# Reordered attention steps, a hand-written order for the memory projection and one low part moved in a decoder-trunk kernel

## The chip, the cores and the metric

The kernel runs on one core of a Trainium2 chip. The metric is the device time of one execution in microseconds (us), and lower is better. The kernel before took 1815.08 us (median of three runs, 1813.99 to 1815.76).

The engines are named as in the profile. PE is the matrix engine and PEld its weight loads, which run beside its matmuls. DVE is the vector engine, ACT the scalar engine, POOL the GpSimd engine. SP issues most of the DMAs. PSUM is the accumulator memory that PE writes.

## The reference, cut to what matters

One inference step of one decoder layer for a prompt of 1024 rows and eight samples of four rows (all float32):

```
h = rms_norm(x) @ w_in                      # u | v | q latent | kv latent | rope key
a = chunk_gmlp(u, v)                        # group A
b = softmax(q k^T / sqrt(96)) v             # group B: 8 heads of 64+32; prompt and samples
x = x + concat(norm(a), norm(b)) @ w_o      # output projection
hm = rms_norm(mem_prompt, g_mem_in)         # 256 memory rows of 1024
mk = rms_norm(hm @ w_mk per head of 128, g_mk)   # output o_mk
mv = hm @ w_mv                                   # output o_mv
x = x + mem_attend(rms_norm(x), mk, mv)
x = x + (silu(conv(gate)) * val) @ w_down   # gate, val = rms_norm(x) @ w_up
```

Three places of this computation are touched: the prompt's attention in group B, the stretch in which mk and mv are computed while the last of the eight sample batches finishes its softmax, and the beginning of the down projection.

## The kernel before

**Products.** A float32 product is made of three PE passes over two-part operands. `split` (lines 192 to 210) makes the high part with a cast on ACT (L200, or L204 with a gain) and the low part as a subtraction on DVE (L201, or L207 with a gain). `mm3` (line 179) issues high times high, high times low, low times high. Where `self.lows` is a list, the low parts are kept back and `flush` issues them later. Most instructions are L185 (`mm3`), L200 and L201, whatever the stage.

**Order.** A planner orders most instructions. Inside a `manual_schedule` block the named engines run in the order in which the program text issues them; `behind(a, b)` puts instruction a behind b in the plan.

**Prompt attention (phase2a, lines 780 to 850).** All engines but SP run in hand order. The work is twelve units of a head and a half of the prompt, each with three or four steps. One step issues in this order: the transposes of exponentials (`trans`, L1031, with a copy on ACT, L1033), the `outs` of earlier units, the scores of a later unit (`scores`, L1009 to L1020: three matmuls into PSUM, a masked maximum on DVE at L1014 or L1018, a multiplication by the row's root at L1020; the exponential L1023 runs on ACT), the low parts kept back, the products with the values (`value`, L1046), and `extra` work for this step. The `outs` hold the copy of a unit's output out of PSUM with a reciprocal (L1053, L1054 on DVE) and its transposes. The two buffers `s` of PSUM are refilled by the scores after the maxima have read them. The norms of q and k (`proj_group`, with `rsqrt_steps` at lines 238 to 270: eleven short operations) are cut into seven steps that stand in `extra`; the last of them multiplies k by its root (L960).

**Memory's stretch (phase2b, lines 1300 to 1322, and mem_kv, line 1579).** Here only SP runs in hand order; PE, ACT and DVE are ordered by the planner. The last sample batch's softmax (`batch_softmax`, line 1462, thirteen parts: norm steps on POOL, scaling, maxima at L1479, a broadcast through PE at L1508 and L1516, a subtraction at L1528, the exponential at L1524) and its products with the cache (`quad_pv`, L1537) interleave with four heads of `hm @ w_mk` (L1605, 24 matmuls each), sixteen units of `hm @ w_mv` (L185, output tile v) and the norms:

```
for h in range(4):
    for i in range(2):
        nc.tensor.matmul(st[:, 2 * h + i : 2 * h + i + 1], sq[h][:, i * P : i * P + P], self.ones[:, :1], ...)   # L1636
...
    nc.tensor.matmul(st[:, 8 + i : 9 + i], acc[z][:, i * P : i * P + P], self.ones[:, :1], ...)                  # L1639
...
    nc.vector.tensor_scalar(dg, self.ident, r[:, h, i : i + 1], None, ALU.mult)                                  # L1657
    nc.tensor.matmul(bc[:, i * P : i * P + P], self.ones, dg, start=True, stop=True)                             # L1658
```

The memory rows are split by `g_mem_in` into mh and ml (L204, L207) just ahead of the first head. The squares of the memory rows are summed by two reduces (L1617). The weights come through `stream` (line 1566): a DMA issued by SP into one of three buffers `raw`, a cast on ACT, a low part on DVE.

**Output projection (mixed, line 1712, and out_proj, line 1755).** `mixed` loads the weight w_o and the mixed rows; `tail` holds the three closing steps of the last sample batch (L1545, L1549, L1561), and `end` the product with w_uv (L1328). `out_proj` runs `end` and then the chunks (0,0), (0,1) and so on.

**Down projection (ffn_down, line 2468, unit, line 2413).** `unit` splits one weight block into high and low; the last piece of the stage before adds PSUM to kept sums (`place`, L2366 and L2368) and so frees the PSUM buffers that the first products d need.

Of the kernel before, what the change touches and what calls it, by code (L numbers as in the profile page):

```python
# [153 lines left out]
class Net:  # L154
# [83 lines left out]
    def rsqrt_steps(self, p, out, ss, scale, e=None, eps=EPS):  # L238
# [5 lines left out]
        x, q, y, a = (self.t(p, [P, n], d, f"rq{k}{n}", 2 if n < 100 else 1)[:w] for k, d in (("x", F32), ("h", F32), ("y", I32), ("a", F32)))  # L244
# [5 lines left out]
        for k in range(2):  # L250
            yield
            o = out if k else y
            if e is nc.vector:
# [6 lines left out]
                e.scalar_tensor_tensor(o, q, 5.0, y, ALU.add, ALU.mult)  # L260
# [411 lines left out]
    def phase2a(self):  # L672
# [75 lines left out]
        spread(tok_s, 4, 11)  # L748
# [4 lines left out]
        extra[2][:0] = preps[0][2:]  # L753
# [27 lines left out]
        with tc.manual_schedule(engines={E.PE, E.Activation, E.DVE, E.Pool}):  # L781
# [57 lines left out]
            for fs in [V] + [outs[t] for t in sorted(outs)] + [[]] * 4:  # L839
# [52 lines left out]
    def proj_group(self, p, pp, hf, i0, i1, s, c, tt=("tp", 4)):  # L892
# [77 lines left out]
        return [alloc] + qk + [lambda: next(it, 0)] * 7, [lambda i=i: part(i, 2) for i in range(i0, i1) if i < 8]  # L970
# [19 lines left out]
    def head_unit(self, p, pp, h, G, s, c):  # L990
# [7 lines left out]
        def scores(e):  # L998
# [9 lines left out]
            for z in range(nc_):  # L1008
# [3 lines left out]
                self.mm3(sv, [(qh[:, tq], ql[:, tq])], [(kh[:, kc], kl[:, kc])])  # L1012
# [166 lines left out]
    def phase2b(self):  # L1179
# [50 lines left out]
        at(last - 4, 3, lambda: self.split(*wk0, raws[0].rearrange("p (k n) -> p k n", k=8)))  # L1230
        for b in range(NB):
# [3 lines left out]
            for r, (k, pos) in enumerate(((12, 0), (13, 0), (14, 0), (14, 3) if b == NB - 1 else (15, 0), (15, 0) if b == NB - 1 else (15, 3), (16, 0), (17, 0), (17, 3), (18, 2), (19, 2), (20, 0), (21, 2), (22, 3))):  # L1235
                f = lambda b=b, r=r: self.batch_softmax(p, ppt, st[b], r, b == NB - 1)
                if n + k <= last:
                    at(n + k, pos, f)
                else:
                    late.append(f)  # L1240
# [15 lines left out]
        def steps(n0, n1):  # L1256
            for n in range(n0, n1):
# [27 lines left out]
                if 0 <= n < last:  # L1285
                    rope = (Q + 1, quads[Q + 1], st[(Q + 1) // 8]) if n % 2 and Q + 1 < NB * 8 else None
                    for f in self.pair_score(p, pp, n, quads[n // 2], st[n // 16], rope):
                        at(n + 1, -1, f)
# [12 lines left out]
        with tc.manual_schedule(engines={E.SP}):  # L1301
# [5 lines left out]
            mem = self.mem_kv(raws, wk0)  # L1307
            for f in late[:3]:
                f()
            next(mem)  # L1310
            steps(last + 1, last + 4)
            for _ in range(5):
                next(mem)
            steps(last + 4, last + 7)
            for f in late[3:]:
                f()
            for _ in range(6):
                next(mem)
            steps(last + 7, last + 16 + LAG)
            for _ in mem:  # L1320
                pass
# [140 lines left out]
    def batch_softmax(self, p, pp, s, r, final):  # L1462
# [28 lines left out]
        elif r == 4:  # L1491
            s["m"] = self.t(p, [P, 2, 32], F32, "mx", 2)
            peak(0, 0, 24)
        elif r == 5:
            s["it"] = norms(24, 32, nc.gpsimd if final else nc.vector)
# [6 lines left out]
        elif r == 8:  # L1502
            scale(nc.vector, 24, 32)
# [10 lines left out]
        elif r == 11:  # L1514
# [4 lines left out]
            if final:  # L1519
                self.less(nc.vector, s)  # L1520
# [20 lines left out]
    def batch_out(self, p, s, part, pp=None, final=False):  # L1541
        nc = self.nc
        if part == 0:
            s["oo"] = self.t(p, [P, 257], F32, "oo", 2)
            nc.scalar.copy(s["oo"], s["o"])  # L1545
# [33 lines left out]
    def mem_kv(self, raws, wk0):  # L1579
# [7 lines left out]
        mh, ml = (self.t(p, [P, 8, 256], FR, x) for x in ("mh", "ml"))  # L1587
        acc = [self.t(p, [P, 256], F32, f"acc{z}") for z in range(2)]
        mr = [r.rearrange("p (k n) -> p k n", k=4) for r in raws[1:3]]
        xs = [(mh[:, k], ml[:, k]) for k in range(8)]  # L1590
        kr, sq = [], []

        for h in range(4):
            w = wk0 if h == 0 else self.stream(I["w_mk"][h], 8, raw=raws[3].rearrange("p (k n) -> p k n", k=8) if h == 1 else None)
            if h == 1:
                self.behind(self.cast, cast)
            yield
            ps = self.t(pp, [P, 512], F32, "b", 2)[:, :256]
            pairs = ((0, 0), (1, 0)), ((0, 1),)
            for z in pairs if h == 0 else (((0, 0), (0, 1)), ((1, 0),)):  # L1600
                for k in range(8):
                    if h == 0 and z is pairs[0]:
                        cast = self.split(*xs[k], mr[k // 4][:, k % 4], self.col("g_mem_in", k))
                    for a, e in z:
                        nc.tensor.matmul(  # L1605
                            ps, w[a][:, k], xs[k][e], start=z[0] == (0, 0) and a + e + k == 0, stop=len(z) == 1 and k == 7
                        )
                    if h == 0 and z is pairs[0] and k % 2:
                        yield
            kr.append(self.t(p, [P, 256], F32, "kr", 4))  # L1610
            nc.scalar.copy(kr[h], ps)
            sq.append(self.t(p, [P, 256], F32, "sq", 4))
            nc.scalar.activation(sq[h], ps, AF.Square)
            yield
        for x, s2 in zip(mr, acc):
            nc.scalar.activation(x, x, AF.Square)
            nc.vector.tensor_reduce(s2, x.rearrange("p k n -> p n k"), AX.X, ALU.add)  # L1617
        yield
        av = [self.t(pp, [P, 512], F32, f"v{i}") for i in range(2)]

        def values(k):
            wh, wl = (x.rearrange("p k n -> p (k n)").rearrange("p (k n) -> p k n", k=2) for x in self.stream(I["w_mv"][k // 2], 8))
            for i in range(2):
                t = slice(i * P, i * P + P)
                x = self.mm3(av[i], [tuple(x[:, t] for x in xs[k + e]) for e in range(2)],
                             [(wh[:, e], wl[:, e]) for e in range(2)], first=k == 0, last=k == 6)
                if k == 4 and i == 0:
                    self.behind(x, self.spread)

        values(0)  # L1630
        yield
        values(2)
        yield
        for h in range(4):
            for i in range(2):
                nc.tensor.matmul(st[:, 2 * h + i : 2 * h + i + 1], sq[h][:, i * P : i * P + P], self.ones[:, :1], start=True, stop=True)  # L1636
# [4 lines left out]
        r2 = self.t(p, [P, 2], F32, "r2")  # L1641
        r = self.t(p, [P, 4, 2], F32, "r")
        four = lambda x: x.unsqueeze(1).broadcast_to([P, 4, 2])
        self.rsqrt(p, rt, st[:, 8:10], 1.0 / 1024)
        nc.vector.tensor_tensor(r2, rt, rt, ALU.mult)
        nc.vector.tensor_tensor(r, st[:, :8].rearrange("p (h i) -> p h i", h=4), four(r2), ALU.mult)
        rf = r.rearrange("p h i -> p (h i)")
        self.rsqrt(p, rf, rf, 1.0 / 128)
        nc.vector.tensor_tensor(r, r, four(rt), ALU.mult)
        yield  # L1650
        values(4)
        yield
        for h in range(4):
            bc = self.t(pp, [P, 512], F32, "b", 2)[:, :256]
            for i in range(2):
                dg = self.t(p, [P, P], F32, "diag", 3)
                nc.vector.tensor_scalar(dg, self.ident, r[:, h, i : i + 1], None, ALU.mult)  # L1657
# [940 lines left out]
```

## Time and profile before

| quantity | value |
| --- | --- |
| median of three runs | 1815.08 us |
| profiled execution, its own time | 1815.49 us |
| its span in the profile | 1813.8 us |
| PE busy | 1791.1 us |
| DVE busy | 1347.4 us |
| ACT busy | 921.0 us |
| POOL busy | 705.9 us |
| mean granted clock of PE | 0.997 |

The span is what the profiler sees of one execution; 1.69 us of the execution's time lie outside it. A granted clock of 1.00 is 2.4 GHz, one of 0.50 is 1.2 GHz. Busy time of different engines overlaps.

### The profile page before, as it was taken

The numbers are of one execution on the slowest core, as the hardware profiler recorded it, in microseconds if no ns is written. First come the engines' busy times: TensorE is split into PE (matmuls) and PEld (weight loads), VectorE is DVE, ScalarE is ACT, GpSimd is POOL, SyncE is SP. The second block draws the span as 40 slices with busy tenths as digits, with TensorE's granted clock in tenths as the row PEclk, the third lists the DMA queues.
The fourth block names the chain that finished last, engine by engine and source line by source line (L and its number), as shares of the span: only waits on it lengthen the run. The fifth ranks groups of instructions, "written<-read, shape, count | busy, mean of one in ns | idle before, by whom it ended". The sixth has DMA issues, their size and how long they took to land.

```text
span 1813.8 us, 39386 instructions
## 1 busy us (share of the span) xinstructions
PE 1791.1 (99%) x14259; PEld 1696.6 (94%) x14259; DVE 1347.4 (74%) x2778; ACT 921.0 (51%) x1931; POOL 705.9 (39%) x858
## 2 busy tenths in 40 slices
PE   9999999999999999999999999999999999999999
PEld 8999777769999999998899989999999999999999
DVE  7864777667678777787644678988888888878664
ACT  7335676766556555565434567433333333344442
POOL 1021656534455445453033001476677767400000
PEclk9999999999999999999999999999999999999999
DMA  8101354558876666663655255122222222584242
GB/s 324 48 18 62 118 184 129 164 164 229 226 206 191 190 186 194 178 190 125 188 157 195 97 169 181 58 95 83 72 71 83 72 83 83 163 319 150 88 147 78
DMA packets 153044, 261.06 MB, mean 144 GB/s; under 512 B 20881, under 2 KB 97394, under 8 KB 152850
## 3 DMA queue, kind: packets, MB, share of 16 engines
q1 hardware_dynamic: 151986, 257.50, 45.8%
q8 instruction: 113, 1.85, 0.5%
q10 hardware_dynamic: 864, 1.05, 0.2%
q14 instruction: 81, 0.66, 0.1%
HBM read 212.66 MB, written 45.82 MB: 143 GB/s over the span
## 4 chain that ended last, share of the span: by engine, by line
PE 77%; DVE 5%; ACT 2%; DMA 1%; issue 1%; POOL 1%; SPq 1%; DVEq 0%; ACTq 0%; POOLq 0%
PE s L185 22%; PE d L185 12%; PE b L185 8%; PE E L185 7%; PE F L185 7%; PE X L185 7%; PE A L185 3%; PE o L1046 2%; PE o L1537 2%; PE tp L1031 1%; PE tp L185 1%; PE s L1422 1%; PE tp L984 1%; PE v L185 1%; PE t L185 0%
## 5 line engine op out<-in xcount | busy, mean ns | idle before, releaser
L185 PE MATMUL s<-w2h,ch 128*128 128x256 f32 x1018 | 302.1, 297 | 0.0
L185 PE MATMUL s<-w2h,cl 128*128 128x256 f32 x1018 | 293.6, 288 | 0.0
L185 PE MATMUL s<-w2l,ch 128*128 128x256 f32 x1018 | 293.1, 288 | 0.0
L185 PEld LDWEIGHTS s<-w2h,ch 128*128 128x128 f32 x1018 | 191.6, 188 | 3.3 <-issue 2.9
L185 PEld LDWEIGHTS s<-w2h,cl 128*128 128x128 f32 x1018 | 191.4, 188 | 0.4 <-DVE rqa L257 0.4
L185 PEld LDWEIGHTS s<-w2l,ch 128*128 128x128 f32 x1018 | 191.8, 188 | 0.0
L1458 DVE TENSOR_REDUCE ss<-sq 128x16 f32<-128x1024 f32 x128 | 155.2, 1213 | 29.2 <-ACT sq L1455 29.1
L1407 POOL TENSOR_TENSOR cl<-cT,ch 128x512 fp32r<-128x512 f32 x64 | 86.2, 1346 | 197.8 <-ACT ch L1403 192.0
L1455 ACT ACTIVATE sq<-s 128x512 f32<-128x512 f32 x128 | 76.4, 597 | 72.3 <-PE s L185 72.2
L200 ACT CAST a<-brb 128x528 fp32r<-128x528 f32 x77 | 48.9, 634 | 114.7 <-PE d L185 111.2
L1452 ACT ACTIVATE sq<-s 128x512 f32<-128x512 f32 x128 | 76.6, 599 | 50.4 <-PE s L185 41.2
L201 DVE TENSOR_TENSOR a<-brb,a 128x528 fp32r<-128x528 f32 x77 | 54.3, 706 | 59.1 <-ACT a L200 58.8
L185 PE MATMUL d<-a,w 128*128 128x264 f32 x768 | 95.5, 285 | 1.2 <-DVE G L2366 1.2
L185 PEld LDWEIGHTS d<-a,w 128*128 128x128 f32 x768 | 94.3, 188 | 1.4 <-issue 1.4
L2233 POOL TENSOR_TENSOR lo<-s,hi 128x1024 fp32r<-128x1024 f32 x20 | 64.2, 3208 | 45.7 <-ACT hi L2232 45.7
L2289 ACT COPY a<-A 128x264 f32<-128x264 f32 x43 | 16.1, 375 | 120.6 <-PE A L185 114.3
L185 PE MATMUL mm<-wlo,xh 128*128 128x256 f32 (+3 forms) x272 | 77.1, 286 | 0.1
L185 PE MATMUL mm<-whi,xh 128*128 128x256 f32 (+3 forms) x272 | 77.1, 285 | 0.0
L185 PE MATMUL mm<-whi,xl 128*128 128x256 f32 (+3 forms) x272 | 76.9, 287 | 0.0
L1403 ACT CAST ch<-cT 128x512 fp32r<-128x512 f32 x128 | 73.6, 628 | 0.2 <-issue 0.2
L2355 POOL TENSOR_TENSOR cv<-cv,row 128x1056 f32<-128x1056 f32 x22 | 65.1, 2958 | 21.0 <-ACT cv L2354 21.0
L185 PE MATMUL d<-a,hi 128*128 128x264 f32 x552 | 72.0, 285 | 0.0
(802 smaller groups left out, 6371.3 us busy)
## 6 DMA issues: line engine op xcount, KB each, us to landing
cT<-cT SPq DMA_DIRECT2D x256, 160.0 KB, 2.7
ck<-ck SPq DMA_DIRECT2D x256, 144.0 KB, 3.5
raw<-w_up SPq DMA_DIRECT2D x44, 512.0 KB, 3.6
wsumd<-wsum SPq DMA_DIRECT2D x26, 512.0 KB, 3.5
actd<-cv SPq DMA_DIRECT2D x44, 264.0 KB, 2.4
brb<-actd SPq DMA_DIRECT2D x44, 264.0 KB, 5.6
wsum<-w_down SPq DMA_DIRECT2D x22, 512.0 KB, 3.7
raw<-wsumd SPq DMA_DIRECT2D x20, 512.0 KB, 3.7
```

The source lines that it names most:

```text
L185: x = self.nc.tensor.matmul(out, l, r, start=first and i == 0, stop=last and i == len(seq) - 1)
L200: first = {"act": nc.scalar.copy, "pool": nc.gpsimd.tensor_copy, "dve": nc.vector.tensor_copy}[eng](hi, src)
L201: low = lambda: nc.vector.tensor_tensor(lo, src, hi, ALU.subtract)
L1046: nc.tensor.matmul(u["o"][g : g + 64, o : o + m * P], s["v"][:, j, h % 4], th[:, z * P : (z + m) * P], start=j == 0, stop=b == len(banks) - 1,
L1403: nc.scalar.copy(d["h"][:, k], src[k])
L1407: (nc.vector if k else nc.gpsimd).tensor_tensor(d["l"][:, k], src[k], d["h"][:, k], ALU.subtract)
L1452: nc.scalar.activation(sq[:, 0], ps[:, :, n0 : n0 + 256], AF.Square)
L1455: nc.scalar.activation(sq[:, 1], pt.rearrange("p (e d) -> p e d", e=2), AF.Square)
L1458: yield lambda: nc.vector.tensor_reduce(s["ss"][:, g0 : g0 + 2].rearrange("p e (z h) -> p z e h", z=2), sq.rearrange("p z e (h d) -> p z e ...
L1537: nc.tensor.matmul(s["o"][j * 32 : j * 32 + 32], S[:, q * 4 + j], d["ck"][:, j, :257], start=q == 0 and j > 0, stop=q == 7)
L2233: eng.tensor_tensor(lo, src, hi, ALU.subtract)
L2355: nc.gpsimd.tensor_tensor(cv, cv, row, ALU.mult)
```

## The change

1. **Attention.** `copy` goes from `outs` into a list of its own that runs behind the maxima of the step. The first half of the last norm steps goes one step earlier (`norm[4:5]` in step 0, `norm[5:]` in step 1); a transposing step of head 0's k goes from `extra[2]` to `outs[3]`, with a flush; the sample rows' norm steps get fixed places. Each norm step flushes the low parts kept back before it runs. The three score matmuls are issued with low q ahead of low k.
2. **Memory's stretch.** PE, ACT and DVE run in hand order as well. Four of the eight splits of the memory rows are made early. The one-column sums and the diagonal broadcasts give way to matmuls with 32 rows of ones and four broadcast matmuls. The two reduces give way to three additions. The norm is computed on 128x256 rows. The last batch's second norm goes from POOL to DVE, its first maximum behind the second head.
3. **Output projection.** `mixed` and the first two chunks run SP and PE in hand order; the loads for chunk 2 and the last closing step move between chunk (0,0) and chunk (0,1), and `end` behind them. Some casts and low parts get a place behind a named instruction.
4. **Down projection.** The fifth unit's low part is put behind the addition L2366.

```diff
-            extra[0][:0] = norm[4:]
-            extra[1][:0] = v1[3:]
-            steps, outs, pend, V = [], {}, [], []
+            extra[0][:0] = norm[4:5]
+            extra[1][:0] = norm[5:] + v1[3:]
+            steps, outs, copies, pend, V = [], {3: [preps[0][2], self.flush]}, {}, [], []
...
                     self.flush_sums()
-                    for f in V:
+                    for f in copies.pop(t, []) + V:
                         f()
...
-                        outs.setdefault(t + 2, []).append(u["copy"])
+                        copies.setdefault(t + 2, []).append(u["copy"])
...
+        def step():
+            if self.lows:
+                self.flush()
+            next(it, 0)
+
-        return [alloc] + qk + [lambda: next(it, 0)] * 7, [lambda i=i: part(i, 2) for i in range(i0, i1) if i < 8]
+        return [alloc] + qk + [step] * 7, [lambda i=i: part(i, 2) for i in range(i0, i1) if i < 8]
...
-                self.mm3(sv, [(qh[:, tq], ql[:, tq])], [(kh[:, kc], kl[:, kc])])
+                for i, (a, b) in enumerate(((qh, kh), (ql, kh), (qh, kl))):
+                    nc.tensor.matmul(sv, a[:, tq], b[:, kc], start=i == 0, stop=i == 2)
...
-        with tc.manual_schedule(engines={E.SP}):
+        with tc.manual_schedule(engines={E.SP, E.PE, E.Activation, E.DVE}):
...
+        for f in six[:3]:
+            f()
+        for k in range(4, 8):
+            self.split(*xs[k], mr[1][:, k % 4], self.col("g_mem_in", k))
+        head(0)
+        late[0]()
+        load(1)
+        lows[1]()
+        load(2)
+        for f in six[3:5]:
+            f()
+        keep(0)
+        head(1)
+        late[1]()
+        lows[2]()
+        load(3)
+        for x in mr:
+            nc.scalar.activation(x, x, AF.Square, scale=unit)
+        late[2]()
+        late[3]()
+        late[4]()
+        lows[3]()
+        six[5]()
+        keep(1)
+        head(2)
+        load(4)
+        lows[4]()
+        self.peak()
+        keep(2)
+        head(3)
+        load(5)
+        keep(3)
+        values(0, 0, 1)
+        lows[5]()
+        late[4]()
+        load(6)
+        values(1, 0)
+        late[5]()
+        late[6]()
+        values(1, 1)
+        late[7]()
+        lows[6]()
+        acc = add()
+        load(7)
+        lows[7]()
+        self.less(nc.vector, self.final)
+        values(2, 0, 1)
+        for z in range(2):
+            for h in range(4):
+                nc.tensor.matmul(
+                    st[32 * h : 32 * h + 32, :256], self.ones[:, :32], acc if z else sq[h], start=z == 0, stop=z == 1
+                )
         for i in range(2):
-            for z in range(2):
-                nc.tensor.matmul(st[:, 8 + i : 9 + i], acc[z][:, i * P : i * P + P], self.ones[:, :1], start=z == 0, stop=z == 1)
+            nc.tensor.matmul(st[:, 256 + i : 257 + i], acc[:, i * P : i * P + P], self.ones[:, :1], start=True, stop=True)
+        late[8]()
+        values(3, 0, 1)
...
+        for _ in self.rsqrt_steps(p, r, st[:, :256], 1.0 / 128, eps=EPS * EPS, room=sq):
+            pass
+        self.rows = self.root
+        self.rsqrt(p, rt, st[:, 256:258], 1.0 / (1024 * unit * unit))
+        seven()
...
+        for h in range(4):
+            nc.tensor.matmul(bc[h], self.ident[:, 32 * h : 32 * h + 1].broadcast_to([P, P]), r, start=True, stop=True)
...
+                    if c:
+                        self.behind(self.cast, self.exp)
+                        self.behind(self.low, self.rows)
...
+        with self.tc.manual_schedule(engines={E.SP, E.PE}):
+            chunk(0, 0)
+            rest()
+            chunk(0, 1)
+            end()
...
+                if z == 0 and k == 4:
+                    self.behind(self.first, self.drained)
```

`values(j, i)` issues six v matmuls per half i of the memory rows, `head(h)` the 24 matmuls of one head of w_mk, `keep(h)` its copy and square on ACT, `load(j)` one weight stream with its cast, `lows[j]` the low part of that weight, `late` and `six` the parts of the last batch's softmax and the sample steps, `seven()` the last batch's products with the cache, `rest()` a closing step and the loads of chunk 2.

## Rows read from the trace of the kernel before

**Rows 1.** The page's first part: engine, busy time, share of the span, instructions.

```profile
PE 1791.1 (99%) x14259; PEld 1696.6 (94%) x14259; DVE 1347.4 (74%) x2778; ACT 921.0 (51%) x1931; POOL 705.9 (39%) x858
```

**Rows 2.** PE's waits: line, tile, releaser, total us, times, longest.

```profile
PE tp L1031 <- ACT pr L1023: 3.0, 5, 1.1
```

**Rows 3.** Stretches: length, busy us of PE, PEld, DVE, ACT, POOL; PE's clock, DMA share, GB/s.

```profile
211.65:215.65 4.00, 2.62 (x14) 1.67 (x13) 2.15 (x5) 2.23 (x6) 1.45 (x2) 1.00 0.50 140
215.65:222.47 6.82, 6.82 (x26) 5.20 (x25) 4.03 (x15) 0.96 (x2) 3.10 (x5) 0.50 0.59 199
846.26:885.83 39.57, 36.48 (x258) 29.65 (x258) 31.61 (x71) 22.99 (x40) 8.84 (x14) 0.96 0.55 172
867.60:871.00 3.40, 3.40 (x27) 3.20 (x26) 1.83 (x3) 1.23 (x2) 0.00 (x0) 1.00 0.79 246
871.00:874.40 3.40, 3.40 (x9) 2.65 (x9) 2.44 (x13) 1.08 (x1) 0.00 (x0) 0.50 0.44 118
```

**Rows 4.** Timeline of DVE, attention: start us, duration us, line, tiles, [idle before <-releaser].

```profile
232.84 0.41 DVE L1053 COPY oc<-o 128x256 f32<-128x256 f32 x1
233.18 0.15 DVE L1054 RECIPROCAL rsum<-rsum 128x4 f32<-128x4 f32 x1
233.26 0.51 DVE L1018 TENSOR_SCALAR_CACHE_REDUCE pr<-s 128x384 f32<-128x384 f32 x1
```

**Rows 5.** Timeline of PE, attention: three of the four stalls.

```profile
233.84 0.47 PE L185 MATMUL s<-kTh,qTh 96*128 96x448 f32 x1 [1.29 <-DVE pr L1018]
...
299.12 1.09 PE L1031 MATMUL tp<-ident,pr 128*128 128x128 f32 x8 [1.11 <-DVE qTl L207]
...
325.93 0.77 PE L1031 MATMUL tp<-ident,pr 128*128 128x128 f32 x5 [0.32 <-ACT pr L1023]
```

**Rows 6.** Timeline of DVE, first steps of attention.

```profile
207.75 1.82 DVE L960 TENSOR_TENSOR k<-k,hr 128x512 f32<-128x512 f32 x2
```

**Rows 7.** Timeline of PE, memory's stretch.

```profile
848.06 0.36 PE L1605 MATMUL b<-mh,wk0h 128*128 128x256 f32 x1 [1.52 <-DVE S L1454]
...
852.34 0.28 PE L1605 MATMUL b<-mh,hi 128*128 128x256 f32 x1
...
855.42 0.39 PE L1605 MATMUL b<-mh,hi 128*128 128x256 f32 x1
...
867.92 0.95 PE L1636 MATMUL st<-ones,sq 128*128 128x1 f32 x8
...
870.49 0.49 PE L185 MATMUL v<-hi,mh 128*128 128x512 f32 x1
...
881.84 1.36 PE L1658 MATMUL b<-diag,ones 128*128 128x128 f32 x8
```

**Rows 8.** Timeline of PE, sums of squares with 32 rows of ones.

```profile
994.86 1.16 PE L1861 MATMUL st<-qsq,ones 128*32 128x256 f32 x8
995.95 0.40 PE L185 MATMUL b<-xh,hi 128*128 128x288 f32 x1
```

**Rows 9.** Timeline of PE, four value products (128 x 64 by 256 columns).

```profile
208.24 0.65 PE L1046 MATMUL o<-pth,v 128*64 128x256 f32 x4
208.82 0.39 PE L185 MATMUL tp<-wvh,ckh 128*128 128x256 f32 x1
```

**Rows 10.** Groups of DVE in memory's stretch: busy us, mean ns, idle before.

```profile
L201 DVE TENSOR_TENSOR lo<-raw,hi 128x1024 fp32r<-128x1024 f32 x8 | 9.7, 1220 | 4.3 <-ACT hi L200 4.0 <-issue 0.3
...
L1617 DVE TENSOR_REDUCE acc<-ck 128x256 f32<-128x1024 f32 x2 | 3.9, 2012 | 0.0
...
L1476 DVE TENSOR_TENSOR S<-S,ss 128x256 f32<-128x256 f32 x1 | 0.4, 426 | 1.1 <-POOL ss L269 1.1
```

**Rows 11.** Timeline of DVE, memory's stretch: a streamed weight's low part.

```profile
876.25 1.23 DVE L201 TENSOR_TENSOR lo<-raw,hi 128x1024 fp32r<-128x1024 f32 x1 [2.42 <-ACT hi L200]
```

**Rows 12.** Timeline of DVE, ahead of the down projection.

```profile
1582.86 0.68 DVE L201 TENSOR_TENSOR hi<-raw,hi 128x512 fp32r<-128x512 f32 x1
```

**Rows 13.** Timeline of PE, start of the down projection.

```profile
1585.37 0.60 PE L185 MATMUL d<-a,w 128*128 128x264 f32 x3 [1.24 <-DVE G L2366]
```

More of the change, by code (lines that the diff above doesn't have):

```diff
@@ L1306, in phase2b @@
             self.wp = self.open("w", bufs=3, side="right")
[L1307 to L1321, printed above, removed]
+            six = [lambda n=n: steps(last + n, last + n + 1) for n in range(1, 7)]
+            self.mem_kv(raws, wk0, m0, late, six, lambda: steps(last + 7, last + 16 + LAG))
         self.close("p3")
@@ L1586, in mem_kv @@
         st = self.t(pp, [P, 512], F32, "st", 1)
-        mh, ml = (self.t(p, [P, 8, 256], FR, x) for x in ("mh", "ml"))
-        acc = [self.t(p, [P, 256], F32, f"acc{z}") for z in range(2)]
+        av = [self.t(pp, [P, 512], F32, f"v{i}") for i in range(2)]
+        ml, mh = (self.t(p, [P, 4, 256], FR, x) for x in ("ml", "mh"))
         mr = [r.rearrange("p (k n) -> p k n", k=4) for r in raws[1:3]]
[L1590 to L1600, printed above, removed]
+        xs = m0 + [(mh[:, k], ml[:, k]) for k in range(4)]
@@ L1601, in mem_kv, with head @@
+        def head(h):
+            ps[h] = self.t(pp, [P, 512], F32, "b", 2)[:, :256]
+            n = 0
+            for z in (((0, 0), (1, 0)), ((0, 1),)) if h == 0 else (((0, 0), (0, 1)), ((1, 0),)):
                 for k in range(8):
-                    if h == 0 and z is pairs[0]:
-                        cast = self.split(*xs[k], mr[k // 4][:, k % 4], self.col("g_mem_in", k))
                     for a, e in z:
-                        nc.tensor.matmul(
-                            ps, w[a][:, k], xs[k][e], start=z[0] == (0, 0) and a + e + k == 0, stop=len(z) == 1 and k == 7
-                        )
@@ L1608, in mem_kv, with keep @@
-                    if h == 0 and z is pairs[0] and k % 2:
-                        yield
+                        nc.tensor.matmul(ps[h], w[h][a][:, k], xs[k][e], start=n == 0, stop=n == 23)
+                        n += 1
+        def keep(h):
             kr.append(self.t(p, [P, 256], F32, "kr", 4))
-            nc.scalar.copy(kr[h], ps)
+            nc.scalar.copy(kr[h], ps[h])
             sq.append(self.t(p, [P, 256], F32, "sq", 4))
-            nc.scalar.activation(sq[h], ps, AF.Square)
@@ L1614, in mem_kv @@
[L1614 to L1623, printed above, removed]
-                t = slice(i * P, i * P + P)
[L1625 to L1636, printed above, removed]
+            nc.scalar.activation(sq[h], ps[h], AF.Square)
+        def values(j, *ii):
+            wh, wl = (pair(x) for x in w[j + 4])
+            for i in ii:
+                t = slice(i * P, i * P + P)
+                self.mm3(av[i], [tuple(x[:, t] for x in xs[2 * j + e]) for e in range(2)],
+                         [(wh[:, e], wl[:, e]) for e in range(2)], first=j == 0, last=j == 3)
@@ L1644, in mem_kv @@
[L1644 to L1657, printed above, removed]
-                nc.tensor.matmul(bc[:, i * P : i * P + P], self.ones, dg, start=True, stop=True)
-            nc.vector.scalar_tensor_tensor(kr[h], kr[h], self.col("g_mk"), bc, ALU.mult, ALU.mult)
-            nc.scalar.dma_start(O["o_mk"][h], kr[h])
-            if h == 1:
-                yield
@@ L1773, in chunk @@
             self.square(self.pm, acc[c][:, :n], res, m)
-        end()
-        for m in range(10):
+        E = mybir.EngineType
+        with self.tc.manual_schedule(engines={E.SP, E.PE}):
+            chunk(0, 0)
+            rest()
+            chunk(0, 1)
+            end()
+        for m in range(1, 10):
             if m == 2:
@@ L2437, in unit @@
         self.split(w[:, 0], w[:, 1], raw)
+        self.first = self.low
         b = self.br[bn, k]
@@ L2546, in build @@
         return
-    mxs, ws = N.mixed(tail)
+    mxs, ws, rest = N.mixed(tail)
     xp = N.open("x", side="right")
@@ L2554, in build @@
     pso = N.open("pso", space=PSUM)
-    N.out_proj(pso, po, mxs, ws, xh, xl, r3, end)
+    N.out_proj(pso, po, mxs, ws, xh, xl, r3, rest, end)
     N.x = xh, xl
```

103 lines of the change are left out of this document (73 added, 30 removed).

## The prediction

> **What bounds the kernel now.** The page's first part comes first: PE is busy 1791.1 us [rows 1] of a span of 1813.8, so all of PE's idle time is 22.7 us, and a change of order can give back little more than its share of that, apart from PE time that a change removes or that runs at the lower clock. The waits of PE show where the idle time lies: the largest entry is the transposes of exponentials, 3.0 us in five waits, none above 1.1 [rows 2]. The stretches of interest then go through the windows view [rows 3]. Two things are to be seen there. Memory's stretch takes 39.57 us, in which PE is busy 36.48 and DVE 31.61: PE bounds it, DVE is close behind. And the clock of PE, 2.4 GHz nearly everywhere, stands at the 1.2 GHz level in two stretches: 6.82 us in attention, after a stretch in which PE was busy 2.62 of 4.00 us, and 3.40 us in memory's stretch, after one in which it was busy all of 3.40. At half the clock these cost 3.4 and 1.7 us, if all the work in them goes at the pace of the clock.
>
> The sum is made against the profiled execution, 1815.49 us (span 1813.8 and 1.69 outside it); that lies 0.41 above the median of 1815.08, and the forecast takes the 0.41 off. About 0.2% (3.6 us) is what a measurement of this kernel can tell from no change.
>
> **Attention.** The copy of a unit's output and its reciprocal stand on DVE ahead of the maximum that frees a score bank; from the copy's start to the maximum's is 0.42 us [rows 4]. PE stalls 1.29 us for such a maximum, and on three more places for exponentials or their transposes that come late, 1.11, 0.32 and a third like the first, 1.10 [rows 5]. The copy behind the maxima shortens these three by 0.42 + 0.32 + 0.42 = 1.16; bounds 0 (another input is as late) and 1.2. At the stall of 1.29 the norm steps of q and k stand in front as well and go to an earlier step: I take 1.0, between 0 and 1.29, as some 0.3 will show up where they land. What the copy now stands ahead of is the product with the values of its step; the transposes that read it come a step later, so its lateness costs nothing; were that cover gone, 0.42 for each unit that is bound by it, with twelve units 5 us at worst.
>
> The multiplication of k (1.82 us on DVE [rows 6]) stands in front of maxima at the start of the steps; the change brings it a step forward, or puts a flush of low parts in front of it. Every flush ahead of a norm step issues nothing new, it only puts low parts ahead of short operations. The transposes of k and its cast on ACT move with it. I take 0 for this and for the order of the three score matmuls: from 0.9 lost to 1.4 gained, since PE idles 1.38 us in the 4.00 around it [rows 3]. Of the clock: before it fell to 1.2 GHz, PE had waited in that stretch [rows 3], and the waits there stay nearly as they are, so I keep the fall; 3.4 us is the price if it goes. Attention: 2.2.
>
> **Memory's stretch, PE.** From 39.57 us go:
> - the wait ahead of the first head, 1.52 [rows 7]: the memory's splits no longer wait behind a maximum;
> - the waits between its matmuls: 852.34 - 848.06 = 4.28 for 24 matmuls, against 855.42 - 852.34 = 3.08 for the second head's 24 [rows 7], so 1.2;
> - the one-column sums, 870.49 - 867.92 = 2.57 [rows 7], with the broadcast L1516 among them, which stays; four more of these matmuls ran earlier and go too, so I take 2.5;
> - the diagonal broadcasts with their waits, from 881.84 to the stretch's end, 885.83, less about 0.2 for two small products that stay: 3.8 [rows 3, 7];
> - the lower clock there, 1.7 [rows 3].
>
> Together 10.7. What comes in: sums with 32 rows of ones over 256 columns. The nearest row has four of them as eight records in 995.95 - 994.86 = 1.09 [rows 8]; eight matmuls are 2.2, and two with one column 0.4 more: 2.6. Four broadcasts of 256 columns at 128 rows: value products of 256 columns take 208.82 - 208.24 = 0.58 for four records [rows 9]; eight records make 1.2 (from 0.6 to 2.2, by the sums' pace). The first head still waits for the four splits that are not made early: half of the 1.2 that eight cost, 0.6. In all 4.4, so 39.57 - 10.7 + 4.4 = 33.3.
>
> **Memory's stretch, DVE and the queues.** DVE loses the reduces, 3.9, gains three additions, 1.2 (as the low part of the first's size), 0.7 and 0.43: 2.3 [rows 10]. The norm on 128x256 is eleven operations of 0.43 [rows 10]: 4.7; it takes the place of fourteen small ones of 0.15 [rows 4], 2.1. The second norm of the batch, from POOL, is eleven of 0.15 to 0.43, I take 0.2: 2.2. Eight diagonals go, at 0.25 (between the same rows) 2.0, and four low parts of the memory rows are made ahead at 0.43: 1.7, in a stretch that PE fills (if not covered there, the 1.7 is lost). That is 31.61 - 3.9 + 2.3 + 4.7 - 2.1 + 2.2 - 2.0 - 1.7 = 31.1 of 33.3: 93%, and now in hand order. I take 1.5 us of new waits for it (0 to 6, as DVE's idle time of before, 39.57 - 31.61 = 8.0, is not its work). POOL loses its part and is not late any more. SP issues the same loads, six weights into three buffers; each waits for a buffer that a low part frees, so DVE's place sets the transfer's; a weight's low part has waited up to 2.42 us for its cast [rows 11]. The output's DMAs on ACT's queue are as many as before, later. The gain here is 39.57 - 33.3 - 1.5 = 4.8.
>
> The output projection follows at once. Chunk (0,1) needs the second chunk's mixed rows, which are cast behind the exponential and made low behind the norm's root; I price that at 0, as all 24 matmuls of chunk (0,0) stand in front, at 2 if that cover is short. The w_uv product moves behind two chunks at no cost.
>
> A page of the Trainium skill, "TensorE: Matmul & The Clock Gate", section "Architectural detail: the array is 16× 32×32, not 1× 128×128", says that ACT and DVE are strict first-in, first-out. Hand order then makes every late operand hold all that is behind it. The row of a low part waiting 2.42 us with nothing passed ahead of it agrees, though there the planner had chosen the order [rows 11].
>
> **Down projection.** The first products wait 1.24 us for the addition that frees their banks [rows 13]. In front of it DVE makes two low parts, of 0.68 each; the fifth unit's is one [rows 12]. Behind the addition it gives about 0.6 (0 to 1.24; the sixth's stays in front). PE needs that unit only after the products of four others: no price.
>
> **Sum.** 2.2 + 4.8 + 0.6 = 7.6; 1815.49 - 7.6 - 0.41 = 1807.5.
>
> **The rivals.**
> 1. The clock in attention does not fall any more: 3.4 us better, 1804.1. For it: waits of the kind that go stood ahead. Against: those of the first steps stay. Chance 0.10.
> 2. The clock in memory's stretch falls all the same: 1.7 worse, 1809.2. In the trace it fell after a stretch in which PE had no idle time, with one-column matmuls in it [rows 3, 7], and I count it as gone with these; broadcast matmuls and waits for DVE might bring it back. Chance 0.13. The page named above, section "What's actually happening", has the lower clock come from an idle engine. By that rule, the one-column matmuls would not be the cause and their removal gives no clock back; the trace differs, 3.40 us busy of 3.40 ahead of the fall.
> 3. The attention part does nothing, because the exponentials on ACT or the pairs of score banks are as late as the maxima: 2.2 worse, 1809.7. For it: four of the waits name ACT. Chance 0.12.
> 4. DVE bounds memory's stretch. If its idle time of 8.0 us stays, the stretch takes 31.1 + 8.0 = 39.1: a gain of 0.5 in place of 4.8, and 1811.8, within 0.2% of before. For it: 93%. Against: 4.3 of the idle was in front of streamed low parts [rows 10], whose casts waited for PE. Chance 0.18.
> 5. Slower: strict order on DVE with late weights. Eight streamed weights (six of the stretch, two of the projection) each make DVE wait 2.42 us [rows 11]: 31.1 + 19.4 = 50.5, which is 10.9 more than before; with 2.8 gained elsewhere, 1815.08 + 8.1 = 1823.2. It decides from about 1.4 us for each weight ((39.57 + 2.8 - 31.1) / 8). Against: the mean of the eight in the trace was 4.3 / 8 = 0.5 [rows 10], with a planner's order. Chance 0.08.
>
> **How the numbers follow.** The forecast has 0.39: 1807.5. Faster by over 0.2% (below 1811.5) are the forecast, rivals 1 to 3 and a third of rival 4: 0.39 + 0.10 + 0.13 + 0.12 + 0.06 = 0.80; the rest of rival 4, 0.12, is within 0.2%; slower 0.08. The range reaches from 1802.0 (rival 1 and 2 us of the bounds) to 1814.0 (rival 4 with 2 us more); rival 5 and a little of the others are left out.
>
> **What would show it.** The waits of PE for exponentials and maxima in attention shrink from four of 0.3 to 1.3 us to under 0.9 each. Memory's stretch, from the last score matmul to the first of the output projection, is 34 to 36 us, with no wait above 1 us ahead of the first head and no stretch at 1.2 GHz. The wait ahead of the down projection is about 0.6. Wrong would be: DVE idle in front of low parts while PE waits for its norm or maxima; a longer start of the output projection, with PE waiting for low parts; the same stalls in attention with ACT named.

## The result and the profile after

The changed kernel takes 1817.38 us (median of 20 runs) against 1814.95 for the kernel before (20 runs): 1.0016 times, with a 95% interval of 1.0010 to 1.0023 (the two medians alone give 1.0013). By the medians it is 2.4 us slower, where 1807.5 was forecast. The profiled execution of the changed kernel took 1816.28 us, 0.8 more than that of the kernel before. The stages below explain these two executions; what the other 1.6 us of the medians consist of is not shown. PE's busy time went down by 3.6 us [rows 1], and its idle time up by more, from 22.7 us to 1814.4 - 1787.5 = 26.9 (span less the page's first part):

```profile
span 1814.4 us, 39362 instructions
...
PE 1787.5 (99%) x14247; PEld 1692.6 (93%) x14247; DVE 1351.2 (74%) x2777; ACT 921.0 (51%) x1931; POOL 696.7 (38%) x844
```

Where the time went is seen when both executions are cut at the same PE instructions: first score product of the prompt, last transposed output copy, first and last score product of the samples, first product of w_o with mixed rows, first product of the memory's attention for samples (L1935 before), first product of the down projection, end. Here is the windows view of the kernel before, cut to the five stages in which something changed or could change (length, then busy time and instructions of PE, PEld, DVE, ACT, POOL, clock, DMA share, GB/s). Memory's stretch begins 0.60 us earlier here than in [rows 3]:

```profile
199.37:400.87 201.50, 192.31 (x1312) 143.51 (x1313) 136.06 (x470) 142.52 (x363) 103.51 (x160) 0.98 0.48 152
401.56:845.66 444.10, 443.12 (x3736) 425.34 (x3734) 333.48 (x645) 260.09 (x578) 215.99 (x337) 1.00 0.69 194
845.66:885.83 40.17, 37.08 (x264) 30.25 (x263) 31.79 (x72) 23.05 (x40) 9.31 (x16) 0.96 0.54 170
885.83:1018.56 132.73, 132.73 (x922) 130.48 (x921) 69.51 (x166) 54.87 (x127) 31.15 (x31) 1.00 0.49 154
1583.24:1813.79 230.55, 225.40 (x1850) 224.99 (x1848) 153.27 (x244) 95.46 (x166) 0.00 (x0) 1.00 0.48 161
```

The same five of the changed kernel, and below them its stretch at 1.2 GHz:

```profile
198.58:399.46 200.88, 190.26 (x1312) 141.13 (x1313) 136.88 (x470) 142.34 (x363) 103.47 (x160) 1.00 0.48 152
400.15:845.14 444.99, 443.60 (x3734) 425.22 (x3732) 334.67 (x644) 261.12 (x582) 215.99 (x336) 1.00 0.68 193
845.14:878.95 33.81, 32.65 (x255) 26.40 (x253) 30.14 (x61) 18.99 (x33) 0.39 (x3) 1.00 0.50 157
878.95:1020.62 141.67, 136.54 (x922) 133.39 (x920) 72.16 (x176) 57.69 (x133) 31.48 (x31) 0.98 0.49 155
1585.35:1814.41 229.06, 225.14 (x1850) 224.93 (x1848) 152.95 (x244) 96.34 (x168) 0.00 (x0) 1.00 0.49 162
...
906.95:913.77 6.82, 6.61 (x23) 6.55 (x24) 1.77 (x6) 2.03 (x7) 1.00 (x1) 0.50 0.60 193
```

Attention gains 0.62 us, the samples' stage loses 0.89 (its instructions are nearly the same; over all profiles of this study it took 443.2 to 446.6 us), memory's stretch gains 6.36, the down projection 1.49. The output projection loses 8.94 us: PE had no idle time in it before (132.73 busy of 132.73), and now has 5.1. All of what memory's stretch gained, and 2.6 us more, is given back at once.

The waits of PE (line, tile, releaser, total us, times, longest), first in the changed kernel, then two of the kernel before:

```profile
PE tp L1069 <- DVE oc L1063: 2.6, 2, 1.5
PE tp L1041 <- ACT pr L1033: 1.6, 3, 0.9
...
PE tp L1069 <- DVE rsum L1064: 1.5, 2, 1.2
PE o L1817 <- ACT n L1814: 1.4, 1, 1.4
PE tp L1041 <- DVE kTl L201: 1.3, 1, 1.3
PE m L1336 <- ACT olT L1577: 1.2, 1, 1.2
PE b L1625 <- ACT mh L204: 1.2, 1, 1.2
PE b L185 <- ACT hi L200: 1.2, 1, 1.2
...
PE s L1022 <- DVE pr L1028: 1.1, 5, 0.4
...
PE b L185 <- ACT vf L1713: 0.7, 1, 0.7
...
PE b L185 <- DVE lo L201: 0.6, 1, 0.6
```

```profile
PE s L185 <- DVE pr L1018: 2.2, 7, 1.3
...
PE tp L1059 <- DVE rsum L1054: 0.3, 1, 0.3
```

The two rows of L1069 are the attention: the transposes of the output copies now wait 4.1 us for copies and reciprocals, against 0.3 in the kernel before. The waits for exponentials (pr on ACT) answer to [rows 2] and fell from 3.0 to 1.6 us, the scores' waits for maxima (pr on DVE) from 2.2 to 1.1. The wait for kTl, a low part of k, is in the attention too. The wait for mh is the one of memory's first head. Five others (n, olT, hi, vf and lo), 5.1 us together, lie in the output projection. Three of them follow from one late load. SP's queue (issue of DMAs: start, duration with waits, line):

```profile
885.84 0.33 SPq L1834 DMA_DIRECT2D res<-res  x1
886.28 8.23 SPq L1787 DMA_DIRECT2D raw<-mix  x4
894.56 1.41 SPq L1830 DMA_DIRECT2D res<-xT  x3
896.08 0.36 SPq L1586 DMA_DIRECT2D raw<-w_o  x1
```

The third block of w_o is issued at 896.08, behind a store and the four loads of chunk 2's rows. Timeline of ACT, DVE and PE around the moment at which PE needs it:

```profile
902.21 1.04 ACT L200 CAST hi<-raw 128x1024 fp32r<-128x1024 f32 x1 [2.85 <-DMA raw<-w_o]
...
900.70 0.14 DVE L264 SCALAR_TENSOR_TENSOR rqy<-rqh,rqy 32x1 f32<-32x1 f32 x1
903.28 1.23 DVE L201 TENSOR_TENSOR lo<-raw,hi 128x1024 fp32r<-128x1024 f32 x1 [2.45 <-ACT hi L200]
904.43 0.96 DVE L259 SCALAR_TENSOR_TENSOR rqa<-rqy 32x1 f32<-32x1 f32 x1
...
903.31 0.44 PE L185 MATMUL b<-mx0h,hi 128*128 128x384 f32 x1 [1.16 <-ACT hi L200]
...
904.57 0.44 PE L185 MATMUL b<-mx0h,lo 128*128 128x384 f32 x1 [0.64 <-DVE lo L201]
...
907.16 0.63 PE L1817 MATMUL o<-ident,n 32*128 32x32 f32 x4 [1.45 <-ACT n L1814]
```

ACT waits 2.85 us for the block, PE 1.16 for the cast and 0.64 for the low part. The low part stands on DVE in the middle of the short operations that make the sample rows' root: the next of these comes at 904.43 in place of about 900.9, where the one before it ends, and the transposes that need n wait 1.45 us. These waits stand directly ahead of the 1.2 GHz stretch; the last of them runs into it.

### The profile page after: what moved, and what is told of

Same layout as the page of the kernel before. It is cut to its first block, busy times and chain, and to the rows that moved or that the text cites. A ratio compares the mean times of both kernels' runs of the same rounds, so it can differ in the third digit from the quotient of the medians.

```text
span 1814.4 us, 39362 instructions
## 1 busy us (share of the span) xinstructions
PE 1787.5 (99%) x14247; PEld 1692.6 (93%) x14247; DVE 1351.2 (74%) x2777; ACT 921.0 (51%) x1931; POOL 696.7 (38%) x844
## 4 chain that ended last, share of the span: by engine, by line
PE 77%; DVE 5%; ACT 3%; DMA 2%; issue 1%; SPq 1%; ACTq 0%; DVEq 0%; POOL 0%
PE s L185 19%; PE d L185 12%; PE b L185 7%; PE E L185 7%; PE F L185 7%; PE X L185 7%; PE A L185 3%; PE s L1022 2%; PE o L1056 2%; PE o L1552 2%; PE tp L1041 1%; PE tp L185 1%; PE s L1430 1%; PE v L185 1%; PE b L1625 1%
```

## The experiments

Each kernel was timed in five rounds with the kernel before on the same chip unless noted; ratios are to the kernel before, with 95% intervals. For comparison: the changed kernel has 1.0016 (1.0010 to 1.0023). The kernel before had medians of 1814.0 to 1814.7 us in these rounds.

**The output projection's part undone**, to see whether the hand order of its chunks is the cause (the edit, cut to the call):

```diff
-        mxs, ws, rest = N.mixed(tail)   # loads, closing steps and chunks in the new hand order
+        mxs, ws = N.mixed(tail)         # mixed and out_proj as before
```

> The changed kernel with the output projection's part undone: loads, closing steps and chunks in the order of before, planned but for SP. Theory A (the changed order of the output projection and ACT's queue at its start give back what memory's stretch gains): the first matmul of the projection stays about 7 us earlier than before, most of it survives to the end, 1806 to 1810 us, ratio near 0.996, and no 1.2 GHz stretch near 907 us. Rival B (the stores on ACT and the late loads give it back in either order): waits of PE of 4 us or more in the first 30 us of the projection, 1813 to 1817 us.

1815.41 us, 1.0007 (0.9998 to 1.0016). In its profile PE waits 3.0 us for olT on ACT and 2.5 for POOL's scaled output, and has 6.8 us at 1.2 GHz from 881.9. So the planner's order gives the gain back too: rival B. What feeds the projection is late in either order, though not by the same operand: here ACT waits 5.44 us for a load of mixed rows, and olT is copied behind the cast of these rows, at 884.24.

**One store of mk, two buffers for the values' copies**, to free ACT's queue:

```diff
-            kr.append(self.t(p, [P, 256], F32, "kr", 4))
+            kr.append(krs[:, h])                      # one tile of [P, 4, 256]
...
-            vf = self.t(p, [P, 512], F32, "vf")
+            vf = self.t(p, [P, 512], F32, "vf", 2)
...
-            nc.scalar.dma_start(O["o_mk"][h], kr[h])
+        nc.scalar.dma_start(O["o_mk"].rearrange("h p m -> p h m"), krs)
```

> The changed kernel with the four stores of mk made one and two buffers for the values' copies. Theory A, in the form that ACT's first-in first-out queue holds the last closing copy (olT) behind two waits for a store and four store issues: that copy comes 3 to 5 us earlier than at 889.7 us, PE's wait ahead of the w_uv product (1.2 us) goes, the casts and so the weight loads behind it come earlier, the waits after chunk (0,2) shrink from 3.2 us to under 1.5, 1808 to 1813 us. Rival C (the weight load of the third block of w_o is late by SP's order and buffers, whatever ACT does): only the 1.2 us go, the wait for its cast stays near 1.2 us, 1815 to 1818 us.

1813.19 us, 0.9989 (0.9979 to 0.9998), 4.2 us less than the changed kernel. What stood in the way is seen on ACT in the changed kernel:

```profile
883.78 0.67 ACT L1713 ACTIVATE vf<-v,rt 128x512 f32<-128x512 f32 x1
884.47 0.37 ACTq L1714 DMA_DIRECT2D o_mv<-vf  x1
886.55 0.69 ACT L1713 ACTIVATE vf<-v,rt 128x512 f32<-128x512 f32 x1 [2.11 <-DMA o_mv<-vf]
887.27 0.34 ACTq L1714 DMA_DIRECT2D o_mv<-vf  x1
887.64 2.05 ACTq L1721 DMA_DIRECT2D o_mk<-kr  x4
889.74 0.21 ACT L1577 COPY olT<-m 128x64 f32<-128x64 f32 x1 [2.50 <-PE b L185]
```

A wait of 2.11 us for the store that empties the single buffer, then 2.05 us for four store issues, and only then the copy, whose input PE had finished at 883.7. With the edit it comes at 885.2 and the wait ahead of the w_uv product is gone. The three waits of the late load stay (1.0, 0.6 and 1.5), and so do 6.8 us at 1.2 GHz; 0.8 for the gain products on DVE stands in place of the 0.7 for vf. So ACT's queue is one cause and the late load another: the time lies 0.2 above theory A's range, the waits are those of rival C. One effect was not meant: the wait of 1.2 us for mh in memory's stretch is gone too, and that stretch takes 32.78 us in place of 33.81.

**The third block of w_o loaded first**, alone:

```diff
             tail[2]()
+            ws[2] = self.stream(I["w_o"][2], 8)
             load((2,))
...
-            if 0 < m < 7:
+            if 1 < m < 7:
```

> The changed kernel with the third w_o block's load ahead of the mixed rows of chunk 2 on SP, nothing else. Theory C (that load is late by its place on SP's queue, in the changed kernel issued at 896.1 us and cast at 902.2): it is issued near 886 us, PE's waits for its cast (1.2 us) and low part (0.6) go, the sample rows' norm on DVE is not held by the low part any more so the wait for n (1.4) goes, and the clock does not fall near 907 us: 5 to 7 us faster than the changed kernel, 1810 to 1813 us. Rival F (another thing is late next: the mixed rows of chunk 2, three buffers later): PE waits 2 us or more in chunk (0,2), 1815 to 1818 us.

1812.81 us, 0.9990 (0.9981 to 0.9999): theory C, 4.6 us less than the changed kernel where 5 to 7 were expected. The block is issued at 886.06, the three waits are gone, and no part of the projection runs at 1.2 GHz:

```profile
878.78:1014.34 135.56, 133.08 (x923) 130.52 (x921) 72.17 (x176) 57.73 (x133) 32.36 (x31) 1.00 0.50 162
```

6.1 us less than in the changed kernel, of which 3.5 are PE's busy time, the price of the lower clock there, and 2.7 idle time. Two waits are left: 1.8 for olT and 0.6 for the gain products on DVE.

**Chunk 2's loads ahead of the first chunk's store**, alone:

```diff
-            chunk(0, 0)
-            rest()
+            chunk(0, 0, rest)    # rest runs between the products and the store
```

> The changed kernel with the loads of chunk 2 issued ahead of chunk (0,0)'s store on SP. Theory G (SP's hand order holds these loads behind the store, which waits for DVE's addition until 885.8 us): the loads start near 881 us in place of 886.3, the third block of w_o follows 3 to 5 us earlier, the waits after chunk (0,2) shrink from 3.2 us to under 1: 1811 to 1814 us. Rival H (the three buffers, not the store, hold the loads: they come free with the low parts at 879 to 885 us, and the casts of these rows wait for ACT's stores anyway): under 1 us earlier, 1816 to 1818 us.

1816.84 us, 1.0015 (1.0006 to 1.0024): rival H. The six loads of mixed rows start at 877.7 us but take 14.5 us to issue, each waiting for one of the three buffers, and the block of w_o follows at 897.2. The store was not what held them: the wait for the cast shrank to 0.2 us, but that for n is 1.8.

**The copies ahead of the maxima again**, all else of the attention part kept:

```diff
-                        copies.setdefault(t + 2, []).append(u["copy"])
+                        outs.setdefault(t + 2, []).append(u["copy"])
```

> The changed kernel with the output copies put back ahead of the maxima; all else of the attention part stays. Theory D (the copies behind the maxima come too late for the transposes that read them, 4.1 us of waits in the profile of the changed kernel): those waits fall under 0.5 us, stalls for maxima come back with 1 to 2 us, 2 to 3 us faster than the changed kernel. Rival E (the prediction's: lateness costs nothing): 1 to 2 us slower than the changed kernel.

1814.92 us, 1.0004 (0.9995 to 1.0013): theory D, 2.5 us less than the changed kernel by the medians, though the two intervals overlap. The attention takes 199.19 us in place of 200.88. The waits for the copies are gone (0.3 is left), and those for exponentials are back; the stalls for maxima are not, against the expectation:

```profile
198.61:397.80 199.19, 190.10 (x1312) 141.22 (x1313) 138.03 (x470) 142.45 (x363) 103.83 (x160) 1.00 0.48 154
...
PE tp L1041 <- ACT pr L1033: 3.9, 6, 1.1
...
PE s L1022 <- DVE pr L1028: 1.1, 5, 0.4
```

So the place of the copies is worth 2.3 us of waits for exponentials and costs 3.8 at the transposes. The shorter stalls for maxima come from the rest of the attention part, not from the copies.

In the changed kernel, one of the places, on PE and then on DVE:

```profile
294.31 0.44 PE L1069 MATMUL tp<-ident,oc 128*128 128x128 f32 x2 [1.48 <-DVE oc L1063]
...
293.84 0.41 DVE L1063 COPY oc<-o 128x256 f32<-128x256 f32 x1
```

**The attention part alone, and the changed kernel without it** (each an edit by whole functions: `proj_group`, `head_unit` and the step lists of phase2a as after, or as before):

> The kernel before with the attention part alone. Theory D: the attention is 1.4 us shorter at its end where the clock does not fall in it, and 2 us longer where it does, so 1813 to 1817 us, ratio 0.999 to 1.001. Rival E (the prediction's): 2.2 us faster at either clock, ratio 0.9988 or lower, and no waits over 1 us at the transposes of the copies.

> The changed kernel without its attention part. Theory D (in the median the attention part gives about nothing, as its waits at the transposes take back the shorter stalls, and the clock's fall comes with either order): 1815.5 to 1818.5 us, as the changed kernel. Rival I (the attention part alone makes the changed kernel slower than before): 1813 to 1815 us.

The part alone: 1815.31 us, 1.0005 (0.9996 to 1.0015). The changed kernel without it: 1815.16, 1.0006 (0.9996 to 1.0015). Neither is clear of no change by itself. That the part as it is does not gain 2.2 us is shown. Whether it costs any is left open by the times: 1815.16 lies between the ranges of theory D and rival I.

**Both kernels once more, one profile each:**

> The changed kernel as it is, once more. If the fall of the clock near 907 us belongs to the waits in front of it, it is there again with 3.4 to 6.8 us at 1.2 GHz, and the stretch from the first projection product to the memory attention's first product is again 139 to 142 us; none in the attention. If it is chance, the fall lies elsewhere or is missing.

> The kernel before as it is, once more. If the fall in the attention belongs to the old order of its steps, there is one of 3.4 to 6.8 us between 210 and 240 us again; if it is chance, none there. Memory's stretch again 40 us, the stretch behind it 132 to 133.

1817.33 and 1815.84 us. The changed kernel's projection took 141.72 us again, with two stretches of 3.4 us at 1.2 GHz, at 887.0 and 910.9; the waits were 2.8 (for the gain products on DVE), 1.4, 0.6 and 0.4. The kernel before had 3.4 us at 1.2 GHz from 233.45 and 3.4 from 871.7, its memory's stretch took 40.29 us, and the projection 132.73 again.

**The parts together:** one store, copies ahead of the maxima, the block of w_o first, loads ahead of the store:

> One store of mk and two buffers for the values' copies, copies ahead of the maxima, the third w_o block's load ahead of chunk 2's rows, and these loads ahead of the first chunk's store. If the causes add up: attention 2.5 us, ACT's queue and the loads 8 to 9 us of what memory's stretch gained are kept: 1806 to 1809 us, ratio 0.995 to 0.997. If one supply bounds the start of the output projection whatever the order: 1811 to 1814 us.

1809.49 us, 0.9971 (0.9958 to 0.9983), between the two expectations. One wait was left in the projection: 1.8 us at the first product of chunk (0,1), for the last gain product of mk on DVE, which frees its bank. The projection took 136.21 us, with 3.4 us at 1.2 GHz from 882.95.

**The same with the memory rows' root on POOL:**

```diff
-        self.rsqrt(p, rt, st[:, 256:258], 1.0 / (1024 * unit * unit))
+        for _ in self.rsqrt_steps(p, rt, st[:, 256:258], 1.0 / (1024 * unit * unit), nc.gpsimd):
+            pass
```

> The combined kernel with the eleven short root operations of the memory rows on POOL (three of them stay on DVE). Theory J (DVE bounds the passage from memory's stretch to the projection: low parts, roots and the four gain multiplications follow each other without a gap from 876 us on, and PE waits 1.8 us for the last of them): that wait falls under 1 us, 1 to 2 us faster than the combined kernel, about 1808. Rival K (POOL's operations take 0.3 us and more, so the values' copies come no earlier and free their banks later): wait of 1 to 2 us for the copies, no gain, 1809 to 1810.

1808.61 us, 0.9969 (0.9956 to 0.9982). The wait of 1.8 is gone (theory J); one of 1.9 for n stands in its place, without a stretch at 1.2 GHz, and the two versions' intervals overlap, so the step's own gain is not shown. Attention and output projection:

```profile
198.74:397.63 198.89, 190.11 (x1312) 141.22 (x1313) 138.33 (x470) 142.24 (x363) 103.42 (x160) 1.00 0.48 154
...
876.23:1011.15 134.92, 132.99 (x922) 130.66 (x920) 71.86 (x169) 57.59 (x133) 34.42 (x39) 1.00 0.50 163
```

**The last one with the old attention:**

> The kernel of the run combined_pool with the attention as before the change (old places of the norm steps, of head 0's k and of the copies, old order of the score matmuls). Theory L (with the copies ahead of the maxima the rest of the attention part is worth 2 us: its stretch took 198.9 us in combined_pool against 200.9 to 201.7 with the old order, which also has a fall of the clock there): a fall of 3.4 to 6.8 us between 210 and 240 us, the stretch 200.9 to 202 us, 1810 to 1812 us. Rival M (the attention part is worth nothing in the median): within 1 us of 1808.6.

1809.01 us, 0.9976 (0.9967 to 0.9986): rival M. This execution had no stretch at 1.2 GHz in the attention, and it took 199.85 us with the old order, against 198.89: 1 us, which the medians of 1809.01 and 1808.61 do not tell apart.

Five runs have intervals wholly below the kernel before: one_store and weight_first, by 1 to 2 us, and combined, combined_pool and pool_no_attn, by 5 to 6.

## Why the prediction was wrong

**The output projection is the step that failed.** "I price that at 0, as all 24 matmuls of chunk (0,0) stand in front, at 2 if that cover is short." The measured term is 8.9 us: 5.1 of waits, 3.5 of PE time at the lower clock (against the run with the block first), and 0.3 besides. I looked for cover for the second chunk's low parts and did not ask what else is due when PE comes to the projection 7 us earlier. The copy of olT (889.74 against 890.79), the casts of chunk 2's mixed rows, whose loads go through three buffers (first cast at 890.68 against 891.06), and the third block of w_o came within about 1 us of the times of before. The block was issued at 896.08, while PE was through with the products ahead of it at 902.1, 5 us earlier than in the kernel before, whose load and first product of this block are:

```profile
897.14 1.18 SPq L1571 DMA_DIRECT2D raw<-w_o  x2
...
907.34 0.33 PE L185 MATMUL b<-mx0h,hi 128*128 128x384 f32 x1
```

The run with this block first got 4.6 us back by moving one load. "The w_uv product moves behind two chunks at no cost" was wrong by 1.2 us, and "the output's DMAs on ACT's queue are as many as before, later" named the queue and not what stands behind it: olT. The stores of the values came 7 us later (884.47 and 887.27 against 877.25 and 880.34). Their wait for the single buffer is not new, ACT had 2.41 us of it before; new is that olT stands behind it.

**Memory's stretch was right and undersized.** Forecast 4.8, measured 6.36. In the prediction's cut, 0.60 us later, the stretch is 33.2, where 33.3 and 1.5 of waits were forecast. The 1.5 us of new waits for DVE did not come: it was busy 30.14 of 33.81 us, and PE's one wait in the stretch names ACT. Its load shows behind the stretch instead, as waits of the second chunk for the gain products: 2.8 us in the second profile of the changed kernel, 1.8 in combined. The sums took 869.98 - 868.51 = 1.5 us in place of 2.6:

```profile
868.51 0.64 PE L1697 MATMUL st<-sq,ones 128*32 128x256 f32 x8
868.97 0.61 PE L1697 MATMUL st<-ck,ones 128*32 128x256 f32 x8
869.51 0.61 PE L1701 MATMUL st<-ones,ck 128*128 128x1 f32 x4
869.98 0.48 PE L185 MATMUL v<-hi,mh 128*128 128x512 f32 x1
```

The wait ahead of the first head went too, but for 1.2 us for the later splits (0.6 was forecast) [rows 7]. No stretch at 1.2 GHz was left there: rival 2 did not happen in this stretch, though the low clock came back behind it. That the one-column products had caused it is not shown: in attn_only they ran at 2.4 GHz from 869.69 on, and the clock fell at 850.23, in the first head.

**Attention was wrong in one step.** "the transposes that read it come a step later, so its lateness costs nothing": they waited 4.1 us. DVE reaches the copy behind the maxima when PE stands at the transposes. The maxima's stalls did shrink, but not by the place of the copies, as the run with the copies ahead has the same 1.1 us. The stall of 1.11 us at 299.12 went; one of 1.28 for a low part of k came at 243.10, which no term of the sum has. PE's idle time tells it without the clock: before 201.50 - 192.31 = 9.2 us, changed 200.88 - 190.26 = 10.6, with the copies ahead again 199.19 - 190.10 = 9.1. The 9.2 is the least of the four profiles with the old order; the others have 9.7, 9.8 and 10.6, those with the changed order 10.4 to 10.6. So the 0.62 us that the stage gained between the two profiles are 2.05 of PE's busy time, by the clock, less 1.4 of idle time; the clock was not in the sum, and without it the stage lost. The clock did what rival 1 says: with the new places of the norm steps none of ten profiles has 1.2 GHz in the attention, with the old ones three of four. The fall was kept in the forecast because the waits ahead of it were to stay, and they did not: from 211.65 to 215.65 PE idled 1.38 us before [rows 3], and in the same four us of the changed kernel, 210.86 to 214.86, it idled 0.53. That this is why the clock stayed up is not shown.

**Down projection:** 0.6 forecast, 1.49 measured: the whole wait of 1.24 [rows 13] and 0.26 of PE's busy time. I had the second low part stay in front of the addition; it did not:

```profile
1584.30 0.70 DVE L2374 TENSOR_TENSOR zz<-F,z 128x528 f32<-128x528 f32 x1
1585.04 0.43 DVE L2437 TENSOR_TENSOR G<-F,zz 128x264 f32<-128x264 f32 x1
1585.38 0.68 DVE L201 TENSOR_TENSOR hi<-raw,hi 128x512 fp32r<-128x512 f32 x1
```

**The slower rival** was built on low parts late by 2.42 us on DVE in memory's stretch. That stretch had none of it; the mechanism showed itself one stage later and for another reason, the place of one load on SP. The Trainium skill's "TensorE: Matmul & The Clock Gate", section "Architectural detail: the array is 16× 32×32, not 1× 128×128", has ACT and DVE strictly first-in, first-out. The trace agrees: a wait of 2.11 us for a store and 2.05 of store issues stood in front of olT on ACT, and a root was held 3.5 us behind a low part on DVE.

## What to carry to other kernels

When a stage gets shorter, list what the next stage reads, with the time at which each load is issued and by which queue it is freed: a stage without a single wait before is no proof that it has slack. A copy moved out of the way of one reader is late for its own: look for the first instruction that reads it on the engine that bounds. Stores issued by a computing engine are part of its queue, with the wait for the buffer they empty.

## What the hardware showed that was not expected

The lower clock was not tied to one place. The same kernel had it at 215.65 for 6.8 us in one execution and at 233.45 for 3.4 in another; the changed kernel at 906.95 for 6.8, or at 887.0 and 910.9 for 3.4 each. It mostly came near waits of PE and, in both profiles of the kernel before, also behind one-column products without any idle time [rows 3, 7]. Neither is enough: combined_pool had a wait of 1.9 us and weight_first one of 1.8 with no fall at all, and attn_only ran the one-column products without one behind them. The cause of a fall stays open. Its price differs with the work: in the projection PE's busy time rose by 3.5 us for 6.8 us at 1.2 GHz, half of the stretch; in the attention by about 2.2 (192.31 against 190.1 in profiles without it).

Eight sums of 32 output rows and 256 columns, 16 records, took 1.0 us, where four of them in the row of the forecast took 1.09 [rows 8]. The single records of the trace tell why. The four matmuls of a group write four different groups of 32 rows, and their records start 0.007 us apart, side by side: two such groups take the 1.0. In [rows 8] three of the four start so, at 994.86, and the fourth by itself at 995.40. The forecast took a price for each matmul from that row, and the group is the unit.
